# Two fused decoder layers on one core: the float32 value product moved to the head of its piece and fed without a copy, and a later plan for the last group's score inputs of layer a

## The chip, the core and the metric

The kernel runs on one NeuronCore of a Trainium2 chip. Five engines work from their own instruction queues: TensorE (PE; its weight loads are listed as PEld), VectorE (DVE), ScalarE (ACT), GpSimd (POOL, hardly used here) and SyncE (SP, which only issues transfers). The metric is the device time of one launch in microseconds (us). Three runs of the kernel before took 752.09, 750.37 and 749.97 us, median 750.37.

## What is computed

A trunk of two pre-norm residual layers on 256 tokens of width 2048, all in float32, 16 heads of width 128. Layer a is latent attention (queries and keys out of low-rank latents, with a rotary part of 64), layer b is block attention, which for 256 tokens and blocks of 256 is plain causal attention with a linear distance penalty (ALiBi). Cut to what matters:

```python
# layer a
q = concat(rms_norm(q_nope), rope(rms_norm(q_rope)))     # per head 128 + 64
k = concat(rms_norm(k_nope), rope(rms_norm(k_rope)))
o = softmax(causal(q @ k.T * 192 ** -0.5)) @ v
x = x + (from_heads(o) * silu(gate)) @ w_out_a
# layer b
s = q @ k.T * 128 ** -0.5 - slope[h] * (q_pos - k_pos)
o = softmax(causal(s)) @ v
x = x + (from_heads(o) * silu(gate)) @ w_out_b
```

## The kernel before

**Precision.** Every large product is made of float32r pieces. A weight block of 512 KB is loaded on SP (`wr`, line 133), ScalarE rounds it to its high part (`wh`, line 147), VectorE subtracts to get the low part (`wl`, line 151), and TensorE adds up high times high, high times low and low times high (line 199 is the helper that records every matmul). There are 4 buffers of `wr`, 4 of `wh` and 3 of `wl`: the load of block n waits on SP until both parts of block n-4 are made.

**Layer a's heads** come in 8 groups of two (`group_a`). A group's projections give q, k, v; three turns (`turn`, 440 ns of estimated cost each, tile `ps_ta`) transpose q, k and the rotary part and cut them into parts (`sf`, `sr`, lines 425 to 431). A head then has three steps (`head_steps`): the scores and the softmax (`ps_s`; line 468 on VectorE, 470 on ScalarE, 473 and 475 on VectorE give the probabilities `sm`); the flip, in which ScalarE copies `sm` as 16-bit planes to `pz` (line 445), SP issues a transposing DMA back into `sm` (line 446), VectorE joins the planes to `pz` (line 452 or 487), and `s2_parts` makes `ph` (ACT, line 494), `pl` (DVE, line 495) and `p` (ACT, line 497); and the value product, four TensorE products into one `ps_o` piece (`s3`), which VectorE gates (`og`, line 509) and which is rounded and split for the output projection (`ohl`, line 510 on ScalarE and 511 on VectorE). Of a head's 256 x 256 scores the last 128 x 128 square is held in float32 and its value product is a float32 one.

**Order.** TensorE's main steps are the projections, in a fixed order. The side steps (turns, scores, flips, value products) are put between them by a planner, `ordered`, with the estimated cost of each step and a lag after each: a step may come once its needs are older than their lag times `SLACK` = 1.3. The lag of a turn is `TU` = 3000 ns. The instructions of ScalarE, VectorE and SP follow from the order in which steps are written out, and each engine works its queue in that order.

**Between the layers.** Output blocks 0 to 3 of layer a (`blk_cols`) run first over heads 0 to 11, with the last group's scores and value products between their steps, then over heads 12 to 15 (four weight loads, called #13 to #16 below, after the first twelve, #1 to #12), and then blocks 4 to 7 (`blk_both`, #17 on). `reload(j)` brings x back (`xt`, four loads of 512 KB, line 806) and, as j = 4, the distances of the ALiBi penalty over the causal mask in `c_sb` (192 KB, line 802), all on SP between the weight loads. `bias` of layer b scales these into `alibi` on ScalarE (line 917).

Of the kernel before, what the change touches and what calls it, by code (L numbers as in the profile page):

```python
# [20 lines left out]
F32 = mybir.dt.float32  # L21
# [7 lines left out]
P = 128  # L29
S = 256  # L30
# [15 lines left out]

PA, PB, LO, TU, TUB, S1, S2A, S2B, S3 = 9000, 6000, 6000, 3000, 10000, 4800, 6000, 9000, 3000
FLB = 4500
SLACK = 1.3
HOLD = 4500  # L50
PACE, PACEB = 600, 3500
# [26 lines left out]
def paired(v):  # L78

    return v.rearrange("p (g l e) -> p g e l", l=2, e=16)  # L80


def lines(v):

    return v.rearrange("p (g l e) -> p g l e", l=2, e=16)


def unpaired(v):

    return v.rearrange("p (g e l) -> p g l e", l=2, e=16)  # L90
# [3 lines left out]
def trunk(ctx: ExitStack, tc, xT, gains, cst, w_in_a, w_q_up, w_kv_up, w_out_a, w_in_b, w_out_b, outT):  # L94
    nc = tc.nc
# [3 lines left out]
    wk = pool("wk", bufs=2)  # L99
# [18 lines left out]
    def work(name):  # L118
        return pw.tile([P, 512], F32, tag="w", name=name)
# [78 lines left out]
    def matmul(*args, **kw):  # L198
        chain(nc.tensor.matmul(*args, skip_group_check=True, **kw))  # L199
# [254 lines left out]
    def head_steps(h, scores, bias, vt, cost, needs, needs_v, after, lag, front, pace=PACE, away=0):  # L454
# [3 lines left out]
        st = {}  # L458
# [17 lines left out]
            st["p"] = sm  # L476

        def s2():
            pz = st["z"] = wk.tile([P, 384], F32, tag="pz", name="pz", bufs=2)
            if away:  # L480
                fly(st["p"], pz, front)
            else:
                flip(st["p"], pz, front)
                s2_parts()
# [5 lines left out]
        def s2_parts():  # L490
            pz = st["z"]
            ph = wk.tile([P, S], F32R, tag="ph", name="ph", bufs=2)
            pl = wk.tile([P, S], F32R, tag="pl", name="pl", bufs=2)
            nc.scalar.copy(ph, pz[:, :S])  # L494
            nc.vector.tensor_tensor(pl, pz[:, :S], ph.bitcast(F32), op=ALU.subtract)
            p1 = wk.tile([P, P], F32, tag="p1", name="p1", bufs=2)
            nc.scalar.copy(p1, pz[:, S:])
            st["t"] = ph, pl, p1

        def s3():  # L500
            po = work("ps_o")
            ph, pl, p1 = st["t"]
            vh, vl, v1 = vt()
            matmul(po[:, :S], vh, paired(ph), start=True, stop=False)
            matmul(po[:, :S], vh, paired(pl), start=False, stop=False)
            matmul(po[:, :S], vl, paired(ph), start=False, stop=False)
            matmul(unpaired(po[:, P:S]), v1, lines(p1), start=False, stop=True)
            og = wk.tile([P, S], F32, tag="og", name="og")
            nc.vector.scalar_tensor_tensor(og, po[:, :S], 0.5, gate_of[h // 2][:, h % 2], op0=ALU.mult, op1=ALU.mult)  # L509
            nc.scalar.activation(lines(ogh[:, h]), unpaired(og), AF.Copy)  # L510
            nc.vector.tensor_tensor(lines(ogl[:, h]), unpaired(og), lines(ogh[:, h].bitcast(F32)), op=ALU.subtract)  # L511
# [176 lines left out]
    heads, turns_of = [], []  # L688


    def group_a(g):
        z = {}
# [64 lines left out]
        def scores(h):  # L757
            def f(ps):
# [4 lines left out]

        proj = blk_rows(w_q_up[:, 384 * g:384 * (g + 1)], lambda: lat_st["x"], q_done)
        proj += blk_rows(w_kv_up[:, 512 * g:512 * (g + 1)], lambda: [x[:, 4:] for x in lat_st["x"]], kv_done, PA)
        turns = [Step(turn(i), 440, TU, proj[-1:], sum((h[:1] for h in heads[2 * g - 4:2 * g - 2]), ()) if g > 1 else (), bank=True)
                 for i in range(3)]
        for h in range(2):
            heads.append(head_steps(2 * g + h, scores(h), lambda: c_sb[:, C_MASK:C_MASK + 384],
# [89 lines left out]
    def group_b(g):  # L859
# [73 lines left out]
        for h in range(4):  # L933
            hb.append(head_steps(4 * g + h, scores(h), bias(4 * g + h), lambda h=h: [x[:, h] for x in z["v"]],
                                 545, [tq, tk], v[-1:] + gate[-1:], [], S2B, nc.vector.tensor_copy, PACEB if g < 3 else PACE, FLB))
        for s in (gate[NC - 1], gate[-1]):
# [104 lines left out]
```

## Time and profile before

| | |
|---|---|
| runs | 752.09, 750.37, 749.97 us; median 750.37 |
| the profiled execution: its time | 748.94 us |
| its span (first to last instruction) | 747.1 us, so 1.8 us lie around it |
| TensorE busy | 739.7 us, 99% of the span, 4766 matmuls |
| VectorE busy | 588.3 us, 79% |
| ScalarE busy | 490.2 us, 66% |
| moved by DMA | 153.13 MB, mean 205 GB/s |

TensorE is busy nearly without a break, so little can be seen in the shares. What has to be read is where a matmul begins later after the one before it than others of its kind do; in the timelines the bracket behind a row gives the idle time before it and what ended that.

### The profile page before, as it was taken

The page shows a single profiled execution, that of the slowest core. Times are in us where ns is not written, and L with a number is a line of the kernel's source. Part 1 is how long each engine was busy: PE and PEld are TensorE (multiplying, and loading weights), DVE is VectorE, ACT ScalarE, POOL GpSimd, SP SyncE. Part 2 cuts the span into 40 slices and gives each one's busy share as a digit, 9 for nine tenths or more (in the row PEclk, how much of TensorE's full clock was granted, in tenths as well). Part 3 has the DMA queues.
Part 4 walks back from the last instruction along what each step waited for, and adds up shares of the span by engine and source line. Part 5 has one row for each costly group of instructions (what it writes and reads, how often), then busy time and mean ns, then how long its engine had stood idle before and what let it go on. Part 6 is the DMA issues. An engine that isn't in the chain of part 4 may idle for free.

```text
span 747.1 us, 13205 instructions
## 1 busy us (share of the span) xinstructions
PE 739.7 (99%) x4766; PEld 689.6 (92%) x4766; DVE 588.3 (79%) x1247; ACT 490.2 (66%) x1043; POOL 0.2 (0%) x4
## 2 busy tenths in 40 slices
PE   9999999999999999999999999999999999999998
PEld 8999999999999999988889888898889988899997
DVE  6988899899998697765788877887778967878563
ACT  7867898888877565456667666675567766665441
POOL 0000000000000000000000000000000000000000
PEclk9999999999999999999999999999999999999999
DMA  8875765666657866666888768886778778767771
GB/s 293 277 208 156 198 172 166 183 157 177 167 179 204 278 218 200 203 198 204 226 226 206 209 184 234 237 207 194 212 223 224 197 212 226 225 202 204 239 223 51
DMA packets 148354, 153.13 MB, mean 205 GB/s; under 512 B 47296, under 2 KB 115520, under 8 KB 148288
## 3 DMA queue, kind: packets, MB, share of 16 engines
q1 hardware_dynamic: 148000, 152.14, 71.7%
q8 instruction: 37, 0.61, 0.3%
q14 instruction: 29, 0.24, 0.1%
q10 hardware_dynamic: 288, 0.15, 0.1%
HBM read 139.68 MB, written 2.10 MB: 190 GB/s over the span
## 4 chain that ended last, share of the span: by engine, by line
PE 92%; DVE 3%; DMA 3%; ACT 0%; issue 0%; SPq 0%; DVEq 0%; ACTq 0%
PE acc L199 85%; PE ps_s L199 4%; DVE wl L151 2%; PE ps_o L199 2%; DMA sm<-pz 1%; PE ps_ta L202 1%; DMA c_sb<-cst 1%; DMA wr<-w_in_a 1%; ACT wh L147 0%; DVE xt L410 0%; PE ps_lt L202 0%; DVE xhl L334 0%; DVE pz L487 0%; PE ps_r L199 0%; DVE og L509 0%
## 5 line engine op out<-in xcount | busy, mean ns | idle before, releaser
L147 ACT ACTIVATE wh<-wr 128x1024 fp32r<-128x1024 f32 (+3 forms) x265 | 288.2, 1091 | 142.4 <-PE acc L199 115.0
L151 DVE TENSOR_TENSOR wl<-wr,wh 128x1024 fp32r<-128x1024 f32 (+3 forms) x265 | 313.6, 1187 | 72.0 <-PE acc L199 39.8
L199 PE MATMUL acc<-wh,xhl 128*128 128x512 f32 (+1 forms) x896 | 260.0, 375 | 0.4 <-ACT wh L147 0.4
L199 PEld LDWEIGHTS acc<-wh,xhl 128*128 128x128 f32 x896 | 168.6, 190 | 21.1 <-ACT wh L147 0.7
L199 PE MATMUL acc<-xhl,wh 128*128 128x256 f32 (+1 forms) x768 | 173.3, 312 | 0.0
L199 PE MATMUL acc<-ohl,wh 128*128 128x256 f32 (+1 forms) x800 | 172.2, 306 | 0.1
L199 PE MATMUL acc<-wl,xhl 128*128 128x512 f32 (+1 forms) x448 | 162.3, 374 | 0.1
L199 PE MATMUL acc<-ohl,wl 128*128 128x256 f32 x512 | 140.4, 274 | 0.2 <-DVE wl L151 0.2
L199 PE MATMUL acc<-xhl,wl 128*128 128x256 f32 x512 | 140.2, 274 | 0.0
L199 PEld LDWEIGHTS acc<-ohl,wh 128*128 128x128 f32 x800 | 130.0, 191 | 6.2 <-DVE ohl L511 0.3
L199 PEld LDWEIGHTS acc<-xhl,wh 128*128 128x128 f32 x768 | 126.3, 191 | 6.6
L199 PEld LDWEIGHTS acc<-ohl,wl 128*128 128x128 f32 x512 | 98.3, 192 | 0.5 <-DVE wl L151 0.5
L199 PEld LDWEIGHTS acc<-xhl,wl 128*128 128x128 f32 x512 | 98.3, 192 | 0.2
L199 PEld LDWEIGHTS acc<-wl,xhl 128*128 128x128 f32 x448 | 84.5, 190 | 10.4 <-DVE wl L151 0.4
L199 PE MATMUL acc<-wh,xt 128*128 128x384 f32 (+1 forms) x192 | 57.4, 356 | 0.0
L470 ACT ACTIVATE sm<-sm,mn 128x128 f32<-128x128 f32 x64 | 29.1, 456 | 13.1 <-DVE mn L468 13.1
L199 PEld LDWEIGHTS acc<-wh,xt 128*128 128x128 f32 x192 | 35.0, 189 | 1.2
L199 PE MATMUL acc<-wl,xt 128*128 128x384 f32 (+1 forms) x96 | 33.6, 350 | 1.3 <-DVE wl L151 1.3
L494 ACT CAST ph<-pz 128x256 fp32r<-128x256 f32 x32 | 12.9, 404 | 18.5 <-DVE pz L487 10.8
L511 DVE TENSOR_TENSOR ohl<-og,ohl 128x256 fp32r<-128x256 f32 x32 | 13.5, 423 | 11.9 <-ACT ohl L510 11.4
L510 ACT ACTIVATE ohl<-og 128x256 fp32r<-128x256 f32 x32 | 13.9, 437 | 12.7 <-DVE og L509 12.7
L410 DVE TENSOR_TENSOR xt<-acc,xt 128x256 f32<-128x256 f32 (+1 forms) x36 | 15.4, 476 | 8.0 <-PE acc L199 8.0
(154 smaller groups left out, 723.1 us busy)
## 6 DMA issues: line engine op xcount, KB each, us to landing
wr<-w_in_b SPq DMA_DIRECT2D x128, 512.0 KB, 4.1
wr<-w_in_a SPq DMA_DIRECT2D x32, 512.0 KB, 4.1
wr<-w_out_a SPq DMA_DIRECT2D x32, 512.0 KB, 4.5
wr<-w_out_b SPq DMA_DIRECT2D x32, 512.0 KB, 4.3
wr<-w_in_a SPq DMA_DIRECT2D x15, 416.0 KB, 5.2
wr<-w_q_up SPq DMA_DIRECT2D x16, 384.0 KB, 3.8
wr<-w_kv_up SPq DMA_DIRECT2D x8, 512.0 KB, 3.9
xt<-xT SPq DMA_DIRECT2D x4, 512.0 KB, 5.3
```

Source lines behind the costliest of these rows:

```text
L147: nc.scalar.activation(self.ordering(self.h)[1], self.ordering(self.raw)[0], AF.Copy)
L151: nc.vector.tensor_tensor(self.ordering(self.l)[1], self.ordering(self.raw)[0], self.ordering(self.h.bitcast(F32))[1], op=ALU.subtract)
L199: chain(nc.tensor.matmul(*args, skip_group_check=True, **kw))
L202: chain(nc.tensor.transpose(*args))
L410: nc.vector.tensor_tensor(lines(y), unpaired(b[:, o:o + n]), lines(y), op=ALU.add)
L470: nc.scalar.activation(sm[:, sl], sm[:, sl], AF.Exp, bias=mn[:, t:t + 1], scale=-1.0, accum_out=rs[:, t:t + 1])
L494: nc.scalar.copy(ph, pz[:, :S])
L510: nc.scalar.activation(lines(ogh[:, h]), unpaired(og), AF.Copy)
L511: nc.vector.tensor_tensor(lines(ogl[:, h]), unpaired(og), lines(ogh[:, h].bitcast(F32)), op=ALU.subtract)
```

## The change

Three edits. `s2_parts` makes no copy `p` any more: 32 ScalarE copies of 128 x 128 go, and the float32 product reads the last third of `pz` itself, which gets four buffers instead of two. In `s3` the float32 product stands first in its piece, then high times high, low times high (of v), and high times the probabilities' low part last. And the turns of group 7, the last of layer a, have the lag `TUL` = 4500 instead of 3000.

```diff
+TUL = 4500
...
-            pz = st["z"] = wk.tile([P, 384], F32, tag="pz", name="pz", bufs=2)
+            pz = st["z"] = wk.tile([P, 384], F32, tag="pz", name="pz", bufs=4)
...
             nc.vector.tensor_tensor(pl, pz[:, :S], ph.bitcast(F32), op=ALU.subtract)
-            p1 = wk.tile([P, P], F32, tag="p1", name="p1", bufs=2)
-            nc.scalar.copy(p1, pz[:, S:])
-            st["t"] = ph, pl, p1
+            st["t"] = ph, pl, pz[:, S:]
...
-            matmul(po[:, :S], vh, paired(ph), start=True, stop=False)
-            matmul(po[:, :S], vh, paired(pl), start=False, stop=False)
+            matmul(unpaired(po[:, P:S]), v1, lines(p1), start=True, stop=False)
+            matmul(po[:, :S], vh, paired(ph), start=False, stop=False)
             matmul(po[:, :S], vl, paired(ph), start=False, stop=False)
-            matmul(unpaired(po[:, P:S]), v1, lines(p1), start=False, stop=True)
+            matmul(po[:, :S], vh, paired(pl), start=False, stop=True)
...
-        turns = [Step(turn(i), 440, TU, proj[-1:], sum((h[:1] for h in heads[2 * g - 4:2 * g - 2]), ()) if g > 1 else (), bank=True)
+        turns = [Step(turn(i), 440, TU if g < 7 else TUL, proj[-1:], sum((h[:1] for h in heads[2 * g - 4:2 * g - 2]), ()) if g > 1 else (), bank=True)
```

The third edit moves rows on all engines between the layers. Line numbers in the rows of after are those of the changed file, one off from those of before. VectorE, from the softmax scaling of head 15 to the low parts of the weights behind head 15's `pl`; before:

```order
L475 TENSOR_SCALAR sm<-sm,ri 128x128
L475 TENSOR_SCALAR sm<-sm,ri 128x256
L509 SCALAR_TENSOR_TENSOR og<-ps_o,gate 128x256
L151 TENSOR_TENSOR wl<-wr,wh 128x1024
L511 TENSOR_TENSOR ohl<-og,ohl 128x256
L452 COPY pz<-sm 128x2x384
L495 TENSOR_TENSOR pl<-pz,ph 128x256
L452 COPY pz<-sm 128x2x384
L151 TENSOR_TENSOR wl<-wr,wh 128x1024
L495 TENSOR_TENSOR pl<-pz,ph 128x256
L151 TENSOR_TENSOR wl<-wr,wh 128x1024 x2
```

There the scaling of head 15 (first two rows) stands ahead of both joins of `pz`. After:

```order
L453 COPY pz<-sm 128x2x384
L474 RECIPROCAL ri<-rs 128x2
L476 TENSOR_SCALAR sm<-sm,ri 128x128
L476 TENSOR_SCALAR sm<-sm,ri 128x256
L496 TENSOR_TENSOR pl<-pz,ph 128x256
L152 TENSOR_TENSOR wl<-wr,wh 128x1024 x2
L453 COPY pz<-sm 128x2x384
L496 TENSOR_TENSOR pl<-pz,ph 128x256
L152 TENSOR_TENSOR wl<-wr,wh 128x1024 x2
```

Now the join of head 14 (first row) stands ahead of the scaling of head 15, and two low parts of weights (#13, #14) behind the join of head 15.

SP, from the transposing DMA of head 14 to the load of the distances; before:

```order
L446 DMA_TRANSPOSE sm<-pz 128x6x128
L133 DMA wr<-w_out_a 128x4x256
L446 DMA_TRANSPOSE sm<-pz 128x6x128
L806 DMA xt<-xT 128x4x256
L133 DMA wr<-w_out_a 128x4x256
L806 DMA xt<-xT 128x4x256
L133 DMA wr<-w_out_a 128x4x256 x2
L806 DMA xt<-xT 128x4x256
L133 DMA wr<-w_out_a 128x4x256
L802 DMA c_sb<-cst 128x384
```

The weight load ahead of `c_sb` is #17. After:

```order
L447 DMA_TRANSPOSE sm<-pz 128x6x128
L134 DMA wr<-w_out_a 128x4x256
L805 DMA xt<-xT 128x4x256 x2
L447 DMA_TRANSPOSE sm<-pz 128x6x128
L134 DMA wr<-w_out_a 128x4x256 x2
L805 DMA xt<-xT 128x4x256
L134 DMA wr<-w_out_a 128x4x256
L805 DMA xt<-xT 128x4x256
L134 DMA wr<-w_out_a 128x4x256
L801 DMA c_sb<-cst 128x384
```

The transposing DMA of head 15 now follows two of the loads of x, and the weight load ahead of `c_sb` is #18.

ScalarE, from the `ph` of head 14 to layer b's first penalty; before:

```order
L494 CAST ph<-pz 128x256
L497 COPY p_3618<-pz 128x128
L147 ACTIVATE wh<-wr 128x1024
L494 CAST ph<-pz 128x256
L497 COPY p_3658<-pz 128x128
L147 ACTIVATE wh<-wr 128x1024 x2
L510 ACTIVATE ohl<-og 128x256
L147 ACTIVATE wh<-wr 128x1024
L510 ACTIVATE ohl<-og 128x256
L917 ACTIVATE alibi<-c_sb 128x384
L147 ACTIVATE wh<-wr 128x1024 x2
```

After, over the same stretch:

```order
L495 CAST ph<-pz 128x256
L148 ACTIVATE wh<-wr 128x1024
L446 COPY pz<-sm 128x768
L148 ACTIVATE wh<-wr 128x1024
L495 CAST ph<-pz 128x256
L148 ACTIVATE wh<-wr 128x1024 x2
L509 ACTIVATE ohl<-og 128x256
L148 ACTIVATE wh<-wr 128x1024
L916 ACTIVATE alibi<-c_sb 128x384
L509 ACTIVATE ohl<-og 128x256
L148 ACTIVATE wh<-wr 128x1024
```

The penalty, which reads the freshly loaded `c_sb`, has moved from behind the `ohl` of head 15 (the second line 510 of before) to ahead of it, and the planes' copy of head 15 (line 446 of after) stands behind the `ph` of head 14 and a weight block.

## Rows read from the trace of the kernel before

**Rows 1.** The page: busy time, share of the span and instructions of TensorE and its loads, and TensorE's granted clock in 40 slices, in tenths.
```profile
PE 739.7 (99%) x4766; PEld 689.6 (92%) x4766; DVE 588.3 (79%) x1247; ACT 490.2 (66%) x1043; POOL 0.2 (0%) x4
PEclk9999999999999999999999999999999999999999
```

**Rows 2.** The page: the chain that ended last, its shares by engine and then by line.
```profile
PE 92%; DVE 3%; DMA 3%; ACT 0%; issue 0%; SPq 0%; DVEq 0%; ACTq 0%
PE acc L199 85%; PE ps_s L199 4%; DVE wl L151 2%; PE ps_o L199 2%; DMA sm<-pz 1%; PE ps_ta L202 1%; DMA c_sb<-cst 1%; DMA wr<-w_in_a 1%; ACT wh L147 0%; DVE xt L410 0%; PE ps_lt L202 0%; DVE xhl L334 0%; DVE pz L487 0%; PE ps_r L199 0%; DVE og L509 0%
```

**Rows 3.** The waits of TensorE over the whole span: us in total, times, longest.
```profile
PE acc L199 <- DVE wl L151: 1.6, 6, 0.3
PE ps_s L199 <- DVE sr L431: 0.4, 1, 0.4
```

**Rows 4.** The timeline of TensorE at one boundary between groups of layer a: start, us from the first start to the last end of the row's instructions, their kind and count, idle time before them and what ended it.
```profile
143.91 0.39 PE L199 MATMUL ps_o<-p,v 128*128 128x128 f32 x2
144.05 0.46 PE L199 MATMUL acc<-wh,xt 128*128 128x512 f32 x1
144.74 0.48 PE L199 MATMUL acc<-wl,xt 128*128 128x512 f32 x1 [0.23 <-DVE wl L151]
```

**Rows 5.** The timelines of ScalarE and, in the last two rows, of VectorE at the same place.
```profile
141.02 0.41 ACT L494 CAST ph<-pz 128x256 fp32r<-128x256 f32 x1 [0.32 <-DVE pz L452]
141.33 0.29 ACT L497 COPY p<-pz 128x128 f32<-128x128 f32 x1
141.53 0.47 ACT L425 ACTIVATE sf<-ps_ta,g_sb 128x256 f32<-128x256 f32 x1
141.90 0.68 ACT L430 ACTIVATE sr<-ps_ta,g_sb 128x512 fp32r<-128x512 f32 x1
142.61 0.75 DVE L431 SCALAR_TENSOR_TENSOR sr<-ps_ta,g_sb,sr 128x512 fp32r<-128x512 f32 x1 [0.33 <-ACT sr L430]
143.47 2.35 DVE L151 TENSOR_TENSOR wl<-wr,wh 128x1024 fp32r<-128x1024 f32 x2
```

**Rows 6.** The groups by line, of ScalarE: count, busy us, mean ns of one.
```profile
L497 ACT COPY p<-pz 128x128 f32<-128x128 f32 x32 | 9.4, 294 | 0.0
L445 ACT COPY pz<-sm 128x768 uint16<-128x768 uint16 x16 | 13.3, 831 | 9.6 <-DVE sm L475 8.5 <-ACT sm L470 0.9
```

**Rows 7.** The timeline of TensorE between the layers: the scores of head 14, a step of the output projection, and the first product of head 12's value piece.
```profile
231.29 0.50 PE L199 MATMUL ps_s<-sr 128*128 128x256 f32 x2 [0.42 <-DVE sr L431]
232.21 0.38 PE L199 MATMUL acc<-ohl,wh 128*128 128x256 f32 x2
232.87 0.28 PE L199 MATMUL ps_o<-ph,vh 128*128 128x256 f32 x1
```

**Rows 8.** The timeline of VectorE between the layers: head 12's join, group 7's k parts, head 14's join, the gating and the split of head 15, the residual sum behind output block 0, and #16's low part.
```profile
230.00 0.60 DVE L452 COPY pz<-sm 128x768 uint16<-128x768 uint16 x1 [1.18 <-DMA sm<-pz]
230.50 0.73 DVE L431 SCALAR_TENSOR_TENSOR sr<-ps_ta,g_sb,sr 128x512 fp32r<-128x512 f32 x1
251.21 0.42 DVE L509 SCALAR_TENSOR_TENSOR og<-ps_o,gate 128x256 f32<-128x256 f32 x1
253.69 0.42 DVE L511 TENSOR_TENSOR ohl<-og,ohl 128x256 fp32r<-128x256 f32 x1 [2.05 <-ACT ohl L510]
255.90 0.69 DVE L410 TENSOR_TENSOR xt<-acc,xt 128x512 f32<-128x512 f32 x1 [0.65 <-PE acc L199]
258.72 1.23 DVE L151 TENSOR_TENSOR wl<-wr,wh 128x1024 fp32r<-128x1024 f32 x1 [2.13 <-ACT wh L147]
```

**Rows 9.** The timeline of SP's queue there: start and length of the issue of the transposing DMAs of heads 12, 14 and 15, of weight loads and of the distances.
```profile
226.46 1.21 SPq L446 DMA_TRANSPOSE sm<-pz  x1
237.93 1.21 SPq L446 DMA_TRANSPOSE sm<-pz  x1
241.10 1.23 SPq L446 DMA_TRANSPOSE sm<-pz  x1
246.19 1.84 SPq L133 DMA_DIRECT2D wr<-w_out_a  x2
248.76 0.38 SPq L133 DMA_DIRECT2D wr<-w_out_a  x1
249.19 1.43 SPq L802 DMA_DIRECT2D c_sb<-cst  x1
```

**Rows 10.** The timeline of ScalarE there: `ohl` of head 15, the penalty, and two weight blocks.
```profile
253.24 0.41 ACT L510 ACTIVATE ohl<-og 128x256 fp32r<-128x256 f32 x1
257.22 0.52 ACT L917 ACTIVATE alibi<-c_sb 128x384 f32<-128x384 f32 x1 [3.57 <-DMA c_sb<-cst]
257.65 1.99 ACT L147 ACTIVATE wh<-wr 128x1024 fp32r<-128x1024 f32 x2
```

**Rows 11.** The DMA view of 222 to 262 us: what was moved, in GB/s, in 40 slices of 1 us, and two of its issues with their size and median time to landing.
```profile
GB/s 9 0 0 0 190 322 186 225 304 253 261 223 17 147 338 167 328 189 120 285 278 137 236 380 384 351 341 338 307 352 349 351 350 356 319 330 168 13 0 249
c_sb<-cst SPq DMA_DIRECT2D x1, 192.0 KB, 8.0
sm<-pz SPq DMA_TRANSPOSE x4, 3.4
```

**Rows 12.** The timeline of TensorE in the first weight blocks behind block 0 (the first row), and near the end of layer b (the second).
```profile
269.59 0.38 PE L199 MATMUL acc<-ohl,wl 128*128 128x256 f32 x1 [0.23 <-DVE wl L151]
681.32 0.90 PE L199 MATMUL acc<-ohl,wh 128*128 128x256 f32 x2
```

**Rows 13.** The timeline of TensorE at the start of the kernel, after its idle first 1.19 us and 34 matmuls that keep it warm: four products of 416 columns in each row.
```profile
4.75 1.73 PE L199 MATMUL acc<-wh,xhl 128*128 128x416 f32 x4
6.84 0.87 PE L199 MATMUL acc<-wh,xhl 128*128 128x416 f32 x4
```

## The prediction

> **What bounds the kernel.** I read the page's busy shares first: TensorE is busy 99% of the span, at a granted clock of full speed, 2.4 GHz, in every slice [rows 1]. The chain that ended last says the same: 92% of it is TensorE, and the rest is VectorE's `wl` and the DMAs of `sm` and `c_sb` [rows 2]. So a microsecond on another engine counts only where TensorE waits for it. Its waits are few: six for `wl` and one for the score parts `sr` [rows 3]. An idle time of 0.23 us understates its cost: at 144.05 a product of 512 columns starts, the next one at 144.74 [rows 4], where two of them are otherwise 0.22 apart (four of 416 in 0.87, [rows 13]); the wait costs 0.47 us. With so little to win, the question is which wait a moved instruction makes longer. That I followed in the timelines of ScalarE, VectorE and SP around the waits, and between the layers, where the order of all of them changes.
>
> **The change, part by part. Order of the products.** The same four products stay in one piece; the float32 one is slow by itself and delays the one behind it wherever it stands. I take nothing, -0.2 to +0.2 us for 32 pieces: none of the waits ends at a value piece now [rows 3].
>
> **The copy.** 32 copies of 0.29 us by their records [rows 6], 0.20 from the start of one to the next instruction (141.33 to 141.53, [rows 5]), are 6.4 us of ScalarE's queue. Nearly all lies beside TensorE's work. What lies on the path is the boundary between two groups of layer a. There the copy stands ahead of `sf` and `sr` of the new group's keys; VectorE waits 0.33 us for that `sr`, then makes its own, then the two low parts, on the first of which TensorE waits until 144.74 [rows 4, 5]. Without the copy all of that starts 0.20 earlier, and 0.20 fits into the 0.33. Five of the six waits on `wl` are such boundaries: 5 x 0.20 = **-1.0 us**, from -0.5 (VectorE's own queue is next late in half of it) to -1.45 (the whole record each time).
>
> **pz in four buffers.** A head's planes may be copied before the value piece of the second head before it is done. Before, `p` let `pz` go early; now it is held until the product. Four buffers pay for that. Near the end of layer b two products take 0.90 us in place of 0.39, behind late `ohl` [rows 12]. Earlier copies and fewer copies may halve that 0.5: **-0.25**, 0 to -0.5.
>
> **The last group's lag.** Here the order tells what moves, and the trace what it costs. The scores of head 14 now come behind the value piece of head 12, and VectorE's `sr` of the keys ahead of head 12's join, so the wait of 0.42 at 231.29 [rows 7], made by a join that waited 1.18 us for its DMA [rows 8], goes. But the softmaxes of heads 14 and 15 come later, and what follows is a chain through three queues that ends in the new place of the penalty.
>
> On TensorE the turn's end is at 226.4. Eight steps of 0.66 [rows 7] make 231.7; head 12's piece ends at 232.9, because its `pl` is later than TensorE; one step and the scores of head 14 end at 234.7. On VectorE the `pl` and low parts of heads 12 and 13 stand ahead of the reduction of those scores, so the scaling of head 14 ends near 240.0 and its transposing DMA issues near 240.7, where it was 237.93 [rows 9]. It lands 3.4 us later [rows 11], at 244.1. Now head 15 waits for head 14, as it did not before: ScalarE's planes' copy of head 15 stands behind head 14's `ph` and a weight block. Join 0.60 [rows 8], `ph` 0.41 [rows 5], a weight block 1.0 [rows 10], the copy 0.83 [rows 6]: the transposing DMA of head 15 issues near **247.0**, where it was 241.10 [rows 9], and lands at 250.4. Then join, `ph` and `pl`, 1.4 us, and the low parts of #13 and #14, 2.35 [rows 5]: 254.2. Load #18 takes the buffer of #14, so it stands on SP until then, and `c_sb` behind it: issued at **254.6**, where it was 249.19 behind #17 [rows 9].
>
> When does it land? Before, it took 8.0 us [rows 11], as weights and x were queued ahead of it and the DMAs moved some 345 GB/s [rows 11]. Now six loads of 0.52 MB and its own 0.2 MB are issued from about 248.3 on, 3.34 MB, 9.7 us at that rate, and the first bytes lag the issue by some 1.9 (3.4 for a transposing DMA that meets little, less 1.5 for 0.52 MB at that rate). That makes **259.9**. The bounds are a landing 3.4 us after the issue (258.0), as a transfer that finds the engines free, and 8.0 (262.6) as before. I take the middle, since fewer loads are ahead than before, but some.
>
> Before, this was harmless: ScalarE had done `ohl` of head 15 at 253.24 and only then waited 3.57 us for `c_sb` [rows 10]. Now the penalty stands ahead of that `ohl`. It starts at 259.9; `ohl` on ScalarE follows 0.43 later, takes 0.40, VectorE's half 0.33, and TensorE's last step of block 0 0.67: block 0 ends at 261.7. Before it ended at 255.9, where VectorE's residual sum starts [rows 8]. That is **+5.8 us** (+3.9 to +8.5), and it contains all that goes and comes ahead of it in this stretch, the wait at 231.29 too, for TensorE has nothing else queued: its order is fixed, and all that follows stands behind head 15's share of block 0. It would get there near 256.0, so some 5.0 us of it are one wait.
>
> Behind it a smaller wait goes: at 269.59 TensorE waits for a low part [rows 12] that was late because VectorE waited 2.13 us for ScalarE [rows 8], which waited for `c_sb`. TensorE's delay gives VectorE and ScalarE time to make up for it: **-0.5** (0 to -0.5).
>
> **The sum:** -1.0 - 0.25 + 5.8 - 0.5 = +4.05. On the profiled execution, 748.94 (its span 747.1 and 1.8 around it), that is 753.0. The median of the runs is 750.37, 1.4 above that execution, so the forecast is 750.37 + 4.05 = **754.4 us**. With the bounds of the landing alone it is 752.5 to 757.1.
>
> **The rivals.** *First, the wait brings a slower TensorE.* A wait of 5.0 us is one that nothing in this trace shows: the longest idle time is the first 1.19 us. At the start, behind that, four products of 416 columns take 1.73 us, and some 2 us later 0.87 [rows 13]: half the pace, that of 1.2 GHz, although the granted clock reads full there [rows 1]. If the wait puts the engine back to that pace and it needs again until about 5.3 us (1.19 to 6.5) to come out of it, half of that is lost: +2.6, 757.0. Against it speaks that no row shows a fall in mid-kernel, and that it may come back sooner. The Trainium skill (TensorE: Matmul & The Clock Gate, the part on the HAM clock gate) says that an idle TensorE is put back to 1.2 GHz and activity releases it again; by that rule this rival holds, and the rows at the start agree with the pace, no row with the fall.
>
> *Second, the new wait is small and cancels the gains.* If the join of head 14 doesn't hold head 15, its DMA issues 3.5 us sooner, near 243.5, and `c_sb` at 251.1; what is queued ahead of it starts earlier by as much, less what the DMAs, busy then, can't move sooner, and I put its landing where it was before, at 257.0. Block 0 then ends at 258.8, +2.9, and the sum is +1.15: 751.5, within what can be told from no change. It decides at a landing of 258.0. For it speaks that my chain has five links with errors of some 0.3 us each, of which most could be shorter; against it, that the order puts `ph` of head 14 ahead of head 15's copy, which no duration undoes.
>
> *Third, faster.* The 192 KB of `c_sb` overtake the loads ahead: issued at 251.1 and 3.4 us on its way, it lands at 254.5, before head 15 is gated, and block 0 ends where it did. Then only gains stand: -1.0 - 0.25 - 0.5 = -1.75, with the wait at 231.29 perhaps 0.5 more: 748.4. Against it: 8.0 us for 192 KB in the trace, last behind larger loads [rows 11].
>
> **How the numbers follow.** The bound that a measurement of this kernel can tell is about 0.3%, 2.25 us: faster is below 748.1, slower above 752.6. The forecast with its bounds has 0.48, the first rival 0.20, both slower: 0.68. The second has 0.20 (the same), the third 0.12; I count all of that as faster, though at 748.4 it lies on the edge. The range leaves out the third and the upper tail of the first: 749.2 to 757.6.
>
> **What would show it.** In the profile after: an idle time of 4 to 6 us on TensorE before its `acc` products of head 15, near 255, ended by VectorE's `ohl`; ScalarE waiting over 5 us for `c_sb` ahead of the penalty; `c_sb` issued near 253.6 and landing near 259; the transposing DMA of head 15 near 246 (all these times are worked out on the clock of before, and the boundaries of the groups put the new trace about 1 ahead of it by then); the five boundary waits shorter by 0.2 us each and none at the scores of head 14; full pace behind the wait, or half of it if the first rival holds. I am wrong if head 15's `ohl` is done before TensorE comes to it.

## The result

The changed kernel takes 761.63 us (median; 762.71, 761.59, 761.68 and 760.48), the kernel before 750.26 (four runs, 749.97 to 752.09). The ratio of the two, with its 95% interval, is 1.0146 [1.0124, 1.0168]: slower, as forecast, but by 11 us where 4 were forecast, and above the top of the range, 757.6. The profiled execution of after took 762.71 us, its span is 760.9, 13.8 longer than that of before.

The page of after: busy times, TensorE's granted clock in 40 slices, and the chain by engine; they answer to [rows 1, 2].

```profile
PE 743.7 (98%) x4766; PEld 692.8 (91%) x4766; DVE 587.9 (77%) x1247; ACT 484.8 (64%) x1011; POOL 0.2 (0%) x4
...
PEclk9999999999999989999999999999999999999999
...
PE 64%; DVE 0%; ACT 0%; DVEq 0%; issue 0%
```

ScalarE has 32 instructions fewer. TensorE is busy 4 us longer with the same 4766 matmuls, and one slice of its clock, around 270 us, reads 8: idle time is not all of the loss. The chain could be followed back only to 266.6 us, where TensorE's longest wait ends, and does not say what made that wait. The waits of TensorE, to be laid beside [rows 3]:

```profile
PE acc L200 <- ACT ohl L509: 5.3, 1, 5.3
PE acc L200 <- ACT wh L148: 3.1, 1, 3.1
PE acc L200 <- DVE wl L152: 1.7, 1, 1.7
PE ps_o L200 <- DVE pz L453: 1.2, 1, 1.2
...
PE acc L200 <- DVE ohl L510: 0.6, 1, 0.6
```

The six small waits for low parts and the one at the scores of head 14 are gone. Of these five the one for `wh` was 0.4 us before, and the others are new. Where they stand, in the timeline of TensorE:

```profile
10.22 0.97 PE L200 MATMUL acc<-wh,xhl 128*128 128x416 f32 x4 [3.08 <-ACT wh L148]
...
147.01 0.38 PE L200 MATMUL acc<-wh,xt 128*128 128x512 f32 x1
...
147.47 0.48 PE L200 MATMUL acc<-wl,xt 128*128 128x512 f32 x1
...
235.46 0.46 PE L200 MATMUL ps_o<-pz,v 128*128 128x128 f32 x2 [1.21 <-DVE pz L453]
...
258.12 0.38 PE L200 MATMUL acc<-ohl,wl 128*128 128x256 f32 x1 [1.66 <-DVE wl L152]
...
266.67 1.04 PE L200 MATMUL acc<-ohl,wh 128*128 128x256 f32 x2 [5.33 <-ACT ohl L509]
267.50 0.42 PE L200 MATMUL acc<-ohl,wl 128*128 128x256 f32 x1
267.71 0.63 PE L200 MATMUL acc<-ohl,wh 128*128 128x256 f32 x2
...
695.59 0.38 PE L200 MATMUL acc<-ohl,wh 128*128 128x256 f32 x1 [0.56 <-DVE ohl L510]
```

The rows at 147 are the boundary of [rows 4], and there is no wait any more. Behind the wait of 5.33 us the same kinds of product that take 0.39 and 0.28 us elsewhere take 1.04 and 0.42. The same matmul (by its count) can be found in both traces, and how much later it starts in after gives the account of the whole span:

| stretch | later in after | forecast |
|---|---|---|
| start: wait of 3.08 for the second weight block, half pace behind it | +3.46 | 0 |
| boundaries of the groups of layer a | -1.08 | -1.0 |
| between the layers | +11.07 | +5.8 - 0.5 |
| rest of layer b, most of it the wait at 695.59 | +0.39 | -0.25 |
| sum | +13.84 | +4.05 |

The first line is not the change's: the loads there are the same in both kernels, and the kernel before, profiled again in another run, waits 1.1 us at that place and not 0.4. The median of the other runs of after is 1.1 below the profiled one as well. Without the start, 10.4 us remain, which agrees with the ratio (0.0146 x 750.26 = 11.0, from 9.3 to 12.6).

The 11.07 between the layers consist of 1.2 at head 12's value piece (235.46), 1.9 for the low part of #13 (258.12), some 0.6 at and around head 14's `ohl`, 5.5 for head 15's `ohl` (266.67), 2.2 of half pace behind it, and -0.5 where the wait at 269.59 [rows 12] is gone. The half pace in the windows of after: stretch, busy time and count of PE, PEld, DVE, ACT and POOL, granted clock, DMA share, GB/s.

```profile
261.00:267.00 6.00, 0.67 (x5) 0.43 (x3) 1.28 (x3) 0.84 (x2) 0.00 (x0) 0.77 0.88 295
267.00:271.20 4.20, 4.20 (x20) 4.08 (x20) 2.67 (x6) 2.38 (x4) 0.00 (x0) 0.52 0.00 0
271.20:275.00 3.80, 3.80 (x36) 3.80 (x35) 2.82 (x6) 2.38 (x4) 0.00 (x0) 1.00 0.43 138
```

From 267.0 to 271.2 the granted clock is 0.52, the 1.2 GHz level, and 20 products are done; afterwards, at full clock, 36 in a shorter stretch. From 266.67 on that is 4.53 us x 0.48 = 2.2 us lost. Where the long wait comes from, in SP's queue of after (compare [rows 9]):

```profile
244.19 1.22 SPq L447 DMA_TRANSPOSE sm<-pz  x1
245.82 0.37 SPq L134 DMA_DIRECT2D wr<-w_out_a  x1
246.26 1.17 SPq L805 DMA_DIRECT2D xt<-xT  x2
249.80 1.23 SPq L447 DMA_TRANSPOSE sm<-pz  x1
...
259.69 0.49 SPq L801 DMA_DIRECT2D c_sb<-cst  x1
```

In VectorE's timeline ([rows 8]): the joins of heads 14 and 15, the low parts of #13 and #14, the residual sum behind block 0:

```profile
247.04 0.61 DVE L453 COPY pz<-sm 128x768 uint16<-128x768 uint16 x1 [1.73 <-DMA sm<-pz]
...
255.42 0.61 DVE L453 COPY pz<-sm 128x768 uint16<-128x768 uint16 x1 [4.54 <-DMA sm<-pz]
...
256.84 2.35 DVE L152 TENSOR_TENSOR wl<-wr,wh 128x1024 fp32r<-128x1024 f32 x2
...
268.60 0.69 DVE L411 TENSOR_TENSOR xt<-acc,xt 128x512 f32<-128x512 f32 x1 [1.53 <-PE acc L200]
```

And in ScalarE's ([rows 10]): `ph` of head 15, the penalty, `ohl` of head 15:

```profile
256.06 0.40 ACT L495 CAST ph<-pz 128x256 fp32r<-128x256 f32 x1 [5.33 <-DVE pz L453]
...
265.77 0.52 ACT L916 ACTIVATE alibi<-c_sb 128x384 f32<-128x384 f32 x1 [4.83 <-DMA c_sb<-cst]
266.20 0.41 ACT L509 ACTIVATE ohl<-og 128x256 fp32r<-128x256 f32 x1
```

Head 15's transposing DMA is issued at 249.80 and lands at 254.97, 5.17 us later, behind two loads of x of which the last lands at 254.21. Head 14's, with nothing in flight ahead of it, takes 2.77. The joined planes are late, so the two low parts are late, so #18's buffer is late, so `c_sb` is issued at 259.69. It lands 6.1 us later (the issues in the DMA view of 240 to 265 us, as [rows 11]):

```profile
c_sb<-cst SPq DMA_DIRECT2D x1, 192.0 KB, 6.1
```

### The profile page after: what moved, and what is told of

Its sections match the earlier page's. It is cut to its first block, busy times and chain, and to the rows that moved or that the text cites. A ratio compares the mean times of both kernels' runs of the same rounds, so it can differ in the third digit from the quotient of the medians.

```text
span 760.9 us, 13165 instructions
## 1 busy us (share of the span) xinstructions
PE 743.7 (98%) x4766; PEld 692.8 (91%) x4766; DVE 587.9 (77%) x1247; ACT 484.8 (64%) x1011; POOL 0.2 (0%) x4
## 4 chain that ended last, share of the span: by engine, by line
PE 64%; DVE 0%; ACT 0%; DVEq 0%; issue 0%
PE acc L200 62%; PE ps_s L200 1%; PE ps_o L200 1%; PE ps_r L200 0%; DVE pl L496 0%; DVE xt L959 0%; ACT ph L495 0%; DVE ohl L510 0%; PE ps_st L200 0%; DVEq L1036 0%
## 5 line engine op out<-in xcount | busy, mean ns | idle before, releaser
L200 PE MATMUL acc<-ohl,wh 128*128 128x256 f32 (+1 forms) x800 | 174.2, 308 | 6.0 <-ACT ohl L509 5.3
L200 PEld LDWEIGHTS acc<-ohl,wh 128*128 128x128 f32 x800 | 131.7, 193 | 12.8 <-ACT ohl L509 5.7
L200 PEld LDWEIGHTS acc<-wl,xhl 128*128 128x128 f32 x448 | 84.6, 190 | 10.4 <-DVE wl L152 0.4
```

## The experiments

The theory after the result: nearly all of the loss comes from the lag of group 7 alone, through the chain of the prediction, and a part of it is half pace behind the long wait. The rivals: that the missing copy or the product order costs something in combination; that the wait is set by the loads of x ahead of head 15's DMA and not by the penalty's place; that head 15 is held by head 14 on ScalarE and VectorE. All ratios are to the kernel before, run on the same chip.

**e1_old_lag:** the change without its third edit.

```diff
-        turns = [Step(turn(i), 440, TU if g < 7 else TUL, ...
+        turns = [Step(turn(i), 440, TU, ...
```

> The changed kernel with the lag of the last group's turns back at 3000, so that only the float32 product's place, the missing copy and the four buffers are left. Theory (the whole loss is made by the later plan; the other parts give 0.2 us at each of five group boundaries): 1.0 to 1.3 us faster than the kernel before, 749.0 +- 0.5, no long wait between the layers. Rival (the product's new place or the longer-held pz costs): no faster than before, 750.3 or more.

Measured 751.57 us, 1.0025 [1.0014, 1.0037]. Some 9 of the 11 us belong to the lag, but the other two edits gain nothing. The boundaries gain 1.07 us, as in after. Elsewhere that is lost. The longest of its waits of TensorE, and then VectorE's timeline there:

```profile
PE ps_s L200 <- DVE sr L432: 1.6, 1, 1.6
```

```profile
232.38 0.60 DVE L453 COPY pz<-sm 128x768 uint16<-128x768 uint16 x1 [1.81 <-DMA sm<-pz]
232.86 0.28 DVE L432 SCALAR_TENSOR_TENSOR sr<-ps_ta,sr 128x128 fp32r<-128x128 f32 x1
```

The wait of [rows 7] has grown from 0.42 to 1.6. Head 12's transposing DMA, with two loads issued 1.3 and 2.6 us ahead of it, lands after 4.75 us where it took 3.52, its join holds VectorE, and the `sr` that the scores need stands behind the join. Another 0.65 comes near 270 us and 0.33 late in layer b.

**e2_lag_only:** the kernel before with `TUL = 4500` for group 7, its copy and product order kept.

```diff
+TUL = 4500
...
+        turns = [Step(turn(i), 440, TU if g < 7 else TUL, ...
```

> The kernel before with the lag of the last group's turns at 4500 and nothing else. Theory (the later plan alone makes the loss): 761 to 764, the penalty again ahead of head 15's ohl, a wait of 4 to 6 us there and half pace behind it. Rival (the loss needs the copies' removal, whose shorter ScalarE queue let the penalty move up): within 2 us of before.

Measured 760.11 us, 1.0128 [1.0107, 1.0149]. The waits of TensorE begin with the same one:

```profile
PE acc L200 <- ACT ohl L511: 5.4, 1, 5.4
```

The interval overlaps that of after, 1.0124 to 1.0168: the lag alone brings the whole loss, as far as can be told, with no help of the other edits.

**e3_penalty_last:** after, with the first penalty held on ScalarE until the `ohl` of head 15 is written.

```diff
+            res["ohl"] = nc.scalar.activation(lines(ogh[:, h]), unpaired(og), AF.Copy)
...
+                if h == 0:
+                    after(a, res["ohl"])
```

> The changed kernel with one dependency more: layer b's first penalty may stand on ScalarE only behind head 15's ohl. Theory (the penalty's wait for the distances makes the wait of 5.3 us, and that wait the half pace behind it): both go, 7.8 us, to 753.8 +- 0.8; the waits for head 12's join and for the low part of #13, 3.2 us together, stay. Rival (head 15 would be late anyway, since its transposing DMA landed at 255.4 of the profiled run): 758 or more.

Measured 756.99 us, 1.0093 [1.0074, 1.0111]. The wait of 5.3 us is gone, which shows that the penalty made it; but 7 us over before remain. TensorE's timeline and the window behind it:

```profile
256.32 0.38 PE L200 MATMUL acc<-ohl,wl 128*128 128x256 f32 x1 [1.35 <-DVE wl L152]
...
260.65 0.88 PE L200 MATMUL acc<-ohl,wh 128*128 128x256 f32 x2 [1.10 <-ACT ohl L509]
```

```profile
261.00:264.00 3.00, 2.92 (x15) 2.89 (x15) 1.63 (x3) 0.00 (x0) 0.00 (x0) 0.55 1.07 362
```

Two short waits, 4.3 us apart, stay, and behind them the clock reads 0.55 again. So the half pace does not need a wait of 5 us. Nor does it come each time: one of the four runs has a mean granted clock of 1.000 over the span and takes 754.16 us, in the range expected; the other three have 0.995 to 0.998 and take 756.49 to 757.86.

**e4_filler:** after, with 80 small matmuls into a tile of their own ahead of head 15's step of block 0, so that TensorE works through most of the wait.

```diff
+        pa = work("ps_keep")
+        for _ in range(80):
+            matmul(pa[:, :P], ones_b, ones_b, start=True, stop=True)
...
```

> The changed kernel with 80 small products of ones (128 columns, bf16, results unused) on TensorE in front of head 15's share of output block 0, that is in the time in which it waits 5.3 us; they take some 4.6 us at the pace of the first such products and delay nothing. Theory (the wait itself costs 5.4, the slower pace behind it 2.4 more): the pace stays full behind the wait, 2.4 us faster than the changed kernel, 759.2 +- 0.6. Rival (the slow rows behind the wait are slow for another reason, such as ScalarE and VectorE catching up): the same 761.6, with rows as slow as before.

Measured 759.94 us, 1.0140 [1.0121, 1.0158], which does not tell it from after. The trace does:

```profile
261.52 4.64 PE L200 MATMUL ps_keep<-ones_b 128*128 128x128 bf16 x80
266.81 0.84 PE L200 MATMUL acc<-ohl,wh 128*128 128x256 f32 x2 [0.65 <-ACT ohl L509]
267.48 0.28 PE L200 MATMUL acc<-ohl,wl 128*128 128x256 f32 x1
```

```profile
267.00:271.20 4.20, 4.12 (x36) 3.93 (x36) 3.28 (x7) 2.83 (x5) 0.00 (x0) 1.00 0.02 5
```

`ohl` comes at the same time, yet the next 4.20 us hold 36 products at a clock of 1.00 where after has 20 at 0.52. Up to the same matmul in layer b that stretch is 2.14 us shorter than in after. The other runs agree: over the span the mean granted clock of after is 0.993 and three times 0.996, that of this kernel 0.998 in the profiled run, which has half pace behind a wait at the start, and 0.999 to 1.000 in the others. In this trace 2.6 us are lost in two other places, near 190 us and at the end, of which the first also falls on the kernel before (e0_before_again).

**e0_before_again:** the kernel before, unchanged, profiled a second time.

> The kernel before once more, for a second trace of it. In the traces so far TensorE waits in the kernel's first 12 us for the second weight block: 0.4 us in the one of before, 0.5 to 3.1 in those of the changed kernel and its variants, which issue the same loads there. If that is chance, this trace may show 0.4 to 3 us there and a time above 748.94 by as much; if it belongs to the variants, it shows 0.4 again.

Measured 750.57 us, 0.9994 [0.9981, 1.0007]. Its waits of TensorE:

```profile
PE acc L199 <- ACT wh L147: 1.1, 1, 1.1
...
PE acc L199 <- DVE wl L151: 2.6, 6, 1.3
```

The 1.1 at the start and one of 1.3 at 191.69 are not in the first trace of before, so neither place says anything of the change.

**e6_both:** e3, and the loads of x held behind head 15's transposing DMA on SP.

```diff
+            after(nc.sync.dma_start(res["x"][:, 4 * j:4 * j + 4], ...), res["fly"])
```

> The run with the penalty behind head 15's ohl, with one dependency more: the four loads of x stand on SP behind head 15's transposing DMA, not two of them ahead of it. Theory (that DMA took 5.6 us because it shared the DMA engines with 1 MB of x issued 2 to 3 us ahead, and through the join it makes #13's low part and head 15 late): it lands within 4 us, the waits for #13's low part (1.4 us) and for head 15's ohl (1.1) go, 2.5 to 3 us faster than that run, 754.2 +- 0.8. Rival (the weight loads ahead of it, which stay, make it late): no faster than 757.0 by over 1.

Measured 756.2 us, 1.0069 [1.0051, 1.0088]. VectorE still waits for head 15's planes:

```profile
255.94 0.60 DVE L453 COPY pz<-sm 128x768 uint16<-128x768 uint16 x1 [5.25 <-DMA sm<-pz]
```

That DMA lands 5.41 us after its issue, no sooner than in after: the weight load #15 is now just ahead of it (issued 249.63, landed 254.80). Taking one load away only puts the next one there; as an account of the whole delay the loads of x fell.

**e12_free15:** e3, and head 15's scaling and planes' copy written ahead of head 14's join and `ph`.

```diff
+                if h == 14:
+                    behind(res["join"], res["scaled"])
...
+            if h == 15 and not away:
+                behind(res["cast"], res["front"])
```

> The run with the penalty behind head 15's ohl, with the order of before for one head more: head 15's scaling stands on VectorE ahead of head 14's join, and its planes' copy on ScalarE ahead of head 14's ph. The lag stays at 4500. Theory (head 15's transposing DMA is late because these two stand behind head 14's landing): it issues some 3 us earlier, the waits for #13's low part and for head 15's ohl (2.5 to 3 us) go, 754.0 +- 0.8; only the wait for head 12's join, 1.3, and its price behind it stay. Rival (that DMA is late because the loads around it slow it, wherever it stands): 756 to 757.

Measured 755.7 us, 1.0067 [1.0040, 1.0093]. SP's queue, and VectorE's join of head 15:

```profile
244.04 0.37 SPq L134 DMA_DIRECT2D wr<-w_out_a  x1
244.47 1.14 SPq L813 DMA_DIRECT2D xt<-xT  x2
245.91 1.23 SPq L449 DMA_TRANSPOSE sm<-pz  x1
```

```profile
253.27 0.61 DVE L455 COPY pz<-sm 128x768 uint16<-128x768 uint16 x1 [4.92 <-DMA sm<-pz]
```

Head 14's DMA is issued at 242.41, so head 15's comes 3.5 us behind it (5.6 in after). But it takes 7.34 us, behind three loads that land at 247.54, 249.53 and 251.59, in the order of their issue, and lands at 253.25, 10.8 behind head 14's issue, as in after (254.97 and 244.19). Freed from what stood ahead on the two engines, it waits for the loads instead.

**e15_free15_first:** e12, and the loads of x and weight load #15 held behind head 15's DMA.

```diff
+            if self is res.get("held"):
+                behind(d, res["fly"])
...
```

> The run that frees head 15 from head 14, with three dependencies more: the loads of x and weight load #15 stand on SP behind head 15's transposing DMA, so that only #14 and the distances are ahead of it. Theory (on SP's queue a transfer lands in its turn: head 15's DMA took 7.3 us there because 1.5 MB of loads were issued in the 2 us ahead of it): it lands within 4 us of its issue, the wait for #13's low part (1.4 us) goes, and with the shorter wait for ohl of head 15 the run is 1.5 to 2.5 us faster than that one, which was 5.0 over before. The wait for head 12's join (0.8 to 1.2 us) and that for ohl right behind head 15's value piece (1.1) stay. Rival (a transposing DMA is slow whenever loads run beside it, ahead or behind): still 6 us or more, no gain.

Measured 752.64 us, 1.0032 [1.0015, 1.0048]; in the ratio some 2.6 us faster than e12. Now `c_sb` comes ahead of head 15's DMA too:

```profile
242.14 0.37 SPq L134 DMA_DIRECT2D wr<-w_out_a  x1
242.58 0.49 SPq L812 DMA_DIRECT2D c_sb<-cst  x1
244.01 1.23 SPq L452 DMA_TRANSPOSE sm<-pz  x1
```

```profile
248.26 0.61 DVE L458 COPY pz<-sm 128x768 uint16<-128x768 uint16 x1 [1.77 <-DMA sm<-pz]
```

It takes 4.22 us, and the wait for #13's low part is gone. With the penalty, the two engines' order and the loads all undone, most of the loss is undone: the interval overlaps that of e1, which has no changed lag.

**e14_lag5000:** after with a lag still longer. In this plan the first penalty falls behind head 15's `ohl` by itself.

```diff
-TUL = 4500
+TUL = 5000
```

> The changed kernel with a lag of 5000 in place of 4500, which lays the score inputs still later, but puts head 15's scaling and planes' copy ahead of head 14's join and ph, and the penalty behind head 15's ohl. Theory (the loss is made by those places in the queues, not by the lateness): no wait of over 2 us between the layers, 751 +- 1.2. Rival (later plans cost in proportion): 760 or more.

Measured 754.03 us (twelve runs, 751.37 to 756.48), 1.0041 [1.0025, 1.0057]. In its profiled run, the fastest of the twelve, no wait of TensorE is above 1.2 us, and ScalarE does the penalty at 263.00, behind head 15's `ohl` at 256.50. The loss is a matter of where a lag puts the penalty and head 15's instructions, and does not grow with it; only the profiled run met the 751 expected, so its trace speaks for the fastest of the twelve. Nine of the other eleven have a mean granted clock of 0.997 to 0.999 where the profiled one has 1.000; worked out from all eleven clocks, slower pace is some 1.2 us of the 2.7 by which the median lies above it. The rest was not found.

**e7_no_copy:** e1 with the four products in their old order, so that only the copy is gone.

```diff
+            matmul(po[:, :S], vh, paired(ph), start=True, stop=False)
+            matmul(po[:, :S], vh, paired(pl), start=False, stop=False)
             matmul(po[:, :S], vl, paired(ph), start=False, stop=False)
+            matmul(unpaired(po[:, P:S]), v1, lines(p1), start=False, stop=True)
```

> The run with the old lag, with the products in the order of before: only the missing copy and the four buffers are left of the change. Theory (the place of the float32 product in its piece is neutral): within 0.4 us of the run with the old lag, 751.5 in its call, that is 0.5 to 1.5 us over before. Rival (the float32 product, first in its piece, holds TensorE at the join where before it would have had the copy's time): 0.5 us or more faster than it.

Measured 752.39 us, 1.0017 [1.0003, 1.0031], not to be told from e1: no cost of the products' order shows, in ratios that are known to some 0.15%.

**e13_two_pz:** e1 with two buffers of `pz` as in before.

```diff
-            pz = st["z"] = wk.tile([P, 384], F32, tag="pz", name="pz", bufs=4)
+            pz = st["z"] = wk.tile([P, 384], F32, tag="pz", name="pz", bufs=2)
```

> The run with the old lag, with two buffers of pz as before. Theory (the four buffers let one transposing DMA of the last group of layer b move up, behind which the last one issues later, and so make the last wait 0.25 us longer): the wait near 684 is again 0.4 instead of 0.67, the rest as in that run, 0.3 us faster. Rival (without the copy pz is held until the value product, so two buffers delay planes' copies in layer a): waits of over 1 us for pz or ps_o, slower than that run.

Measured 757.09 us, 1.0085 [1.0064, 1.0105]. The first of TensorE's waits, at 687.13 us:

```profile
PE ps_o L200 <- DVE pz L488: 4.1, 1, 4.1
```

Without the copy `pz` is held until its product is done, and two buffers are too few for the last heads of layer b. The two more buffers are worth 4.5 us (0.6% of 750) there, and a part of that is half pace behind the wait: the granted clock is 0.50 from 689 to 691 us.

**e10_rotary_first:** e1, and VectorE's low part of group 7's rotary keys ahead of head 12's join.

```diff
+                    if g == 7:
+                        for join in res["joins"][12:]:
+                            after(join, low)
```

> The run with the old lag, with one dependency more: on VectorE the low part of group 7's rotary keys stands ahead of head 12's join, which waits for its DMA. Theory (the scores of head 14 wait 1.6 us for that low part only because it is queued behind the join): that wait goes, 1.6 us faster than the run with the old lag, about 0.4 us slower than before if the start of the kernel is alike, 750.0 +- 0.6. Rival (head 12's value piece then waits for the join instead, by as much): 751.5, the wait moved to ps_o.

Measured 750.92 us, 1.0011 [0.9996, 1.0026]. The wait of 1.6 at the scores is gone; waits of 0.34 and 0.46 at the value pieces stand in its place.

**e11_rotary_xt:** e10 and e6's edit to the loads of x.

```diff
+            after(nc.sync.dma_start(res["x"][:, 4 * j:4 * j + 4], ...), res["fly"])
```

> The kernel of the run before this one, with the loads of x on SP behind head 15's transposing DMA, and so the distances ahead of them. Theory (the two waits of 0.3 us for low parts behind block 0 come from ScalarE waiting for the distances): these go too, 1.0 us faster than that run and 0.5 to 1 us faster than the kernel before, 749.0 +- 0.6. Rival (the loads of x, now later, are late for the residual sums, or the waits come from VectorE's own queue): no faster than the run before this one.

Measured 750.71 us, 1.0000 [0.9986, 1.0013]: the time of before.

**e16_merged:** e11, with the scaling of head 12 ahead of a low part and head 13's join behind head 12's `pl`.

```diff
+            if h == 12 and not away:
+                behind(res["low"], s)
...
+                if h == 13:
+                    behind(res["joins"][-1], res["pl12"])
```

> The best guess at a version: no copy, float32 product first, four buffers, the old lag; the rotary low part ahead of head 12's join; head 12's scaling ahead of the weight's low part, so that head 12's transposing DMA has one load less ahead of it; head 12's pl ahead of head 13's join; the loads of x behind head 15's transposing DMA. Theory (what the parts other than the lag lose is all made by head 12's DMA, which lands 1.2 us later than before behind one load more): the waits at head 12's value piece and at head 14's scores go, and the gain of 1.0 us at the group boundaries is left: 749.5 beside 750.5 of before. Rival (the next late thing takes its place, such as head 13's join): no faster than before.

Measured 752.64 us, 1.0043 [1.0027, 1.0058]. TensorE now waits for the low part that was moved back, at 225.26:

```profile
PE acc L200 <- DVE wl L152: 2.6, 1, 2.6
```

Behind that wait, too, the pace is halved: the granted clock is 0.50 from 227 to 230 us.

No version was faster than the kernel before.

## Why the prediction was wrong

**Order of the products, the copy.** Forecast 0 and -1.0; measured no difference that can be told (e7 beside e1) and -1.08 (-1.07 in e1). The working by steps of 0.20 held: the five boundaries give 0.15 to 0.27 each, 0.95 together, and in e2, which keeps the copies, the five waits are still there. What the prediction did not see is that heads' DMAs meet the weight loads elsewhere when a turn comes earlier: head 12's takes 4.62 us in after and 4.75 in e1 against 3.52, and the places where that ends in a wait take back the gain (e1). In after it shows as the wait of 1.21 at 235.46. The cause of the longer landing was read from what is queued ahead and not tested by itself.

**pz in four buffers.** Forecast -0.25 at the end of layer b, measured +0.39 with a wait at 695.59. In after and e1 the third of the last group's four transposing DMAs is issued close behind the second and the fourth later; in before they come in two pairs. That these buffers are needed was right, and is worth 4.5 us (e13).

**The last group's lag.** The mechanism was right in its links, and the lag alone makes the loss (e2): the join of head 14 ahead of head 15's scaling, `c_sb` behind #18, the penalty ahead of head 15's `ohl`, one wait of some 5 us (forecast 5.0, measured 5.33 idle). On the clock of before (2.38 us taken off after's times) its times were:

| | forecast | measured |
|---|---|---|
| issue of head 14's transposing DMA | 240.7 | 241.8 |
| its landing | 244.1 | 244.6 |
| issue of head 15's transposing DMA | 247.0 | 247.4 |
| its landing | 250.4 | 252.6 |
| issue of `c_sb` | 254.6 | 257.3 |
| its landing | 259.9 | 263.4 |
| TensorE comes to head 15's share of block 0 | 256.0 | 259.0 |
| that share begins | 261.0 | 264.3 |
| end of block 0 | 261.7 | 266.2 |

Two agreements in it are luck. That the wait is 5.33 and not 8 us long is so because TensorE came to it 3.0 us later than forecast, held by waits that the forecast did not name, while `ohl` was 3.3 later. And head 15's DMA was issued only 0.4 late because head 14's, 1.1 late, landed sooner after its issue than the 3.4 assumed.

The step that failed is the landing of head 15's transposing DMA, "and lands at 250.4": 3.4 us after its issue, the median of four such transfers [rows 11], although SP's order of after, ahead of the prediction, shows two loads of x between head 14's and it. It took 5.17. On SP's queue every transfer of this stretch lands in the order of issue, and the time of this one went with what was ahead: 2.77 us with nothing in flight (head 14's in after), 5.17 behind the loads of x, 7.34 in e12, 4.22 in e15. The Trainium skill (DMA: Bandwidth & Descriptors, "Queues, rings and completion order") says that each DMA engine takes the descriptors of one ring in their order, though a later transfer may complete before an earlier one; the traces agree with the first, as all 338 transfers of SP land in the order of issue in each of them, and show no case of the second.

What is ahead is not all of it. In after and e12 alike the DMA lands 3.7 us behind the first load of x (251.27 to 254.97, and 249.53 to 253.25), with only the second between them, where loads that follow one another land 1.5 apart (#15 and #16 in after: 256.49 and 257.97). So its own turn takes some 2.2 us, an estimate from these times, while `c_sb`, of the same 192 KB, lands 0.5 behind the load ahead of it (265.23 to 265.75). In a part of that time hardly anything moves, though loads are queued, and the load directly ahead is late too: the second of x lands 2.95 us behind the first, and in e6 #15, with next to nothing ahead of it (`c_sb` lands 0.13 us behind its issue), takes 5.17 where #14 takes 3.66. In after (the columns of the windows above; the last is GB/s):

```profile
252.00:253.00 1.00, 1.00 (x11) 1.00 (x11) 0.00 (x0) 0.00 (x0) 0.00 (x0) 1.00 2.93 117
253.00:254.00 1.00, 1.00 (x11) 1.00 (x11) 0.00 (x0) 0.00 (x0) 0.00 (x0) 1.00 0.05 5
```

No run isolates this pause, and its cause stays open. On the way to the end of block 0, 1.8 us come from the failed step; 0.4 from the issue, 0.5 more on the way to `c_sb`, and 0.8 from its landing, 6.1 us against an estimated 5.3: 3.5 in all. The landing of `c_sb` at 263.4 is later than the upper bound given for it, 262.6.

Ahead of the long wait stand three that the forecast did not name (1.2, 1.9 and 0.6 us in the account above). They don't come on top of its +5.8, which spans the whole stretch. The last two stay in e3, e6 and e12, in each of which head 15's planes land late; in e15, where they land sooner, the low part's is gone.

**Behind the wait.** The prediction gave "the wait brings a slower TensorE" 0.20 and 2.6 us. It came true: 2.2 by the granted clock, 2.14 by e4, where TensorE works through the wait. The sum, which put this term at nothing, was short by it. The Trainium skill (TensorE: Matmul & The Clock Gate, the part on the HAM clock gate) says that an idle TensorE falls to 1.2 GHz and activity releases it, and the trace agrees (0.52, and 1.00 from 271.2 on). "No row shows a fall in mid-kernel" was no evidence against it, since no row of before showed a long wait in mid-kernel either. Of the third rival, which did not come, the sum gives 748.6, or 748.1 with the whole 0.5, and not 748.4; nothing rests on it.

**The range.** 3.5 us of late landing, 2.2 of half pace and 0.6 at the end of layer b make the difference of 6.3 between the account without the start, 10.4, and the forecast's 4.05. Each of the first two was foreseen as a possibility by itself, as a bound of the landing (to 757.1) and as a rival (757.0). The range was made for one or the other. Together they give 757.1 + 2.6 = 759.7, which is nearer to the measured 761.6 than either.

**Left open:** the pause in the DMA engines ahead of a transposing DMA's landing; the rest of what lifts the runs of e14 above its profiled one; why the pace falls behind short waits in some executions and not in others (it fell in the profiled run of e3 and not in those of e6 and e12, with waits of like length, and within e3 and e6 too the mean granted clock differs from run to run, 0.995 to 1.000 and 0.998 to 1.000); and which of e16's further edits gains anything.

## What to carry to other kernels

The time that a transfer took to land here went with the queue in front of it and with its own turn: read it from what the new order puts ahead, load by load, and not from the median of its kind. Where an instruction that waits for a late transfer moves ahead of one that the bounding engine needs, its place can cost more than the edit's own work wins (here 5.5 us and 2.2 behind it, against 1.1), and a dependency that holds it back (e3) recovers only its own share, since the transfers that made it late still delay others. Bounds that can come true together belong added in the range.

## What was not expected of the hardware

Behind two waits of 1.35 and 1.10 us, with TensorE busy between them, its granted clock was 0.55 from 261 to 264 us in e3's profiled run, and behind a single one of 2.6 us it was 0.50 in e16's, while in e6's, with 1.44 and 1.10, it stayed at 1.00. The first microseconds vary between executions: the wait for the second weight block was 0.4, 1.1 and 3.1 us in three traces with the same loads there, and the pace behind the longest of them was halved again (four products of 416 columns, 0.87 us in [rows 13], took 1.59 at 11.81 us and 1.45 at 13.89).
